# Earlier loads in the opening and an untouched memory input: one decoder layer on one core

## The chip, the cores and the metric

The kernel runs on one core of a Trainium2 chip. The core has a tensor engine (PE, with its weight loads shown as PEld), a vector engine (DVE), a scalar engine (ACT), GpSimd (POOL) and a sync engine (SP), which here issues most DMAs. Each engine works through its own instructions in a fixed order and waits, where it must, on semaphores of the others. The metric is the device time of one execution in microseconds (us); the median over several executions is compared.

## The reference

One layer of a hybrid decoder for a prompt of 1024 tokens and 8 sample tokens (1032 columns together), model width 1024, in float32. What matters here:

```python
def rmsnorm(x, w, eps=RMS_EPS):
    xf = x.astype(jnp.float32)
    y = xf * lax.rsqrt(jnp.mean(xf * xf, axis=-1, keepdims=True) + eps)
    return (y * w.astype(jnp.float32)).astype(x.dtype)
...
    sc_b, sc_c, sc_x, z, xbc, dt_raw, q, gates = jnp.split(xn @ w_in, splits, axis=-1)
...
    xbc_c = jax.nn.silu(xbc_c + ssm_conv_b)
...
    dt = jax.nn.softplus(dt_raw.astype(jnp.float32) + ssm_dt_bias.astype(jnp.float32))
    a = -jnp.exp(ssm_a_log.astype(jnp.float32))
...
        mem_n = rmsnorm(mem_prompt, norm_mem_w[l])
        mk = (mem_n @ w_mem_k[l]).reshape(bp, MEM_LEN, ATTN_HEADS, ATTN_HEAD_DIM)
        mv = (mem_n @ w_mem_v[l]).reshape(bp, MEM_LEN, ATTN_HEADS, ATTN_HEAD_DIM)
```

`xn` is the normalized input. It is multiplied by the columns of `w_in`; of these the change touches z (a SiLU gate), xBC (a causal convolution of width 4, which for the sample tokens needs the stored histories) and dt. Keys and values come from 256 normalized memory tokens.

## The kernel before

Matrices are cut into blocks of 128 columns. A product in full precision is made from three products in a faster type: a number is split into a rounded part (tile names ending in h, made by a copy on ACT) and the rest (ending in l, made by a subtraction on DVE), and h·h, h·l and l·h are added up in PSUM. One block of 128 output columns is `gemm`: 8 slices of the inner dimension, three products each, 24 groups; a group is three matmuls of 512, 256 and 264 columns (L220). `weights` (L159) loads a block of weights into a tile with the tag `raw`, of which there are three, and splits it.

*Opening* (L447 to L608). The rows of x come in by DMA in three thirds (`g3` = 0, 1, 2). PE turns each 128x128 block (`ps_xt`), ACT copies it to `xt` (five buffers), SP stores that to `xT_d`, DVE scales it into `xw`, ACT and DVE split it into `xnh` and `xnl`. Products with the dt columns (`ps_dt`) and with the first block of B (`ps_B0`) run among this. Behind the opening come the histories: four DMAs, 32 small transposes (`ps_h`) and four copies on DVE (L610 to L622).

*The next stage* (L1245 to L1253). The block C0 is multiplied (`ps_C`), then z0 and z1 (`z_step`, L854), then pairs of z blocks by a Strassen scheme (`z_pair`, tiles named Z2, Z4 and so on, L266). At the same time DVE and ACT have four things to do: the convolutions of B0 and C0 (`conv`, L745); the sums and differences of quarters of xn that the Strassen scheme needs (`make_raw` and `make_forms`, L1217 to L1234; tiles T1, nT2, T4 and `raw3`); the splitting of weights; and the chain for dt: `dtr` (bias added, read from `ps_dt`), softplus in some twenty operations on [128, 288] (`dt_softplus`), which ends in `dtT` and `da`, and then on PE `ps_ac` (running sums of `da`, `dt_sums`), `ps_acT` (`dt_rows`) and `ps_ex` (`dt_sample`).

*Memory tokens* (L1263 to L1317). Two tiles of 128 tokens are loaded, squared and summed on ACT, multiplied by the root of their mean square on DVE, turned by PE (`mem_t`, `ps_mt`), and each 128x128 piece is scaled by `norm_mem_w` and split, by ACT for the h part and by DVE for the l part. `kv_block` multiplies them with the key and value weights (`ps_kv`) and ACT copies the result out.

The order on each engine is decided when the program is built: a scheduler takes the program in the order in which it was written, plays it through with its own estimates of durations, and puts on each engine whatever is ready by these. Steps in the list `pend` (the dt chain, the memory steps) are written into the products by `tick`, between slices. `tc.issue_after(ins)` is a rule for this scheduler: what is written in the block comes, on the engine of `ins`, behind `ins`.

Two tiles of three PSUM banks (`mm_ps`, tag mm) serve the big products. `ps_dt` and `ps_B0` hold both through the opening; `ps_C` gets one when `dtr` has read `ps_dt` or the copy `uB` has read `ps_B0`, and z0 and z1 get the next ones.

Of the kernel before, what the change touches and what calls it, by code (L numbers as in the profile page):

```python
# [17 lines left out]
P = 128  # L18
# [29 lines left out]
def tile_kernel(ctx: ExitStack, tc, a, o):  # L48
# [123 lines left out]
    def ev_tile(name, shape=(P, TT + 4), dt=F32):  # L172
        return ev.tile(list(shape), dt, tag="ev", name=name)
# [289 lines left out]
    with tc.tile_pool(name="p0", bufs=1) as p0:  # L463
# [123 lines left out]
        root_of(0)  # L587
        for g3 in range(3):
            c, n_all = span(g3)
            for k in range(KD):  # L590
                ps = sm_ps(f"ps_xt{g3}{k}")
                blocks(g3, ps, lambda i, t, n: t[:, k * P : (k + 1) * P])
                ins = to_xn(k, c, ps, n_all, f"{g3}{k}")
                if g3 < 2 and 1 <= k < 1 + len(srcs[g3 + 1]):
                    with tc.issue_after(ins):
                        square(g3 + 1, k - 1)
                if g3 == 0 and k == 2:
                    first_weights()
                if g3 > 0 or k > 3:
                    products.popleft()()  # L600
                if g3 < 2 and k == 5:
                    root_of(g3 + 1)
        while products:
            products.popleft()()
        for k in range(KD):
            b_product(2, k)

        SY.dma_start(r_d, rbc[0:1, :])  # L608


    for src, dst, nr, nt in (
        (a["state_ssm_conv"][0].rearrange("b j c -> (b j) c"), h_xc, 24, 24),
        (a["state_conv"][0].rearrange("b j c -> (b j) c"), h_sc, 16, 8),
    ):
        per = 8
        for q0 in range(0, nt, per):
            t = ev_tile(f"hist{nr}_{q0}", (nr, per * P))
            SY.dma_start(t, src[:, q0 * P : (q0 + per) * P])
            ps = sm_ps(f"ps_h{nr}_{q0}")
            for i in range(per):  # L620
                PE.transpose(ps[:, i * nr : (i + 1) * nr], t[:, i * P : (i + 1) * P], ident[:nr, :nr])
            V.tensor_copy(dst[:, q0 : q0 + per, :].rearrange("p a b -> p (a b)"), ps[:, : per * nr])  # L622
# [16 lines left out]
    bias = pd_.tile([2 * HEADS, 1], F32, tag="bias", name="bias")
    V.memset(bias, 0.0)  # L640
    SY.dma_start(bias[:HEADS], a["ssm_dt_bias"].rearrange("l h -> h l"))
    dtr = ev_tile("dtr", (2 * HEADS, TT))
    V.tensor_scalar(dtr[:, :TT], flat(ps_dt)[: 2 * HEADS], bias, None, op0=ALU.add)
# [10 lines left out]
    def dt_softplus():  # L654
        ps = sm_ps("ps_dtT")
        for c in range(NCK):
            PE.transpose(
                ps[:, c * 2 * HEADS : (c + 1) * 2 * HEADS], dtr[:, c * P : (c + 1) * P], ident[: 2 * HEADS, : 2 * HEADS]
            )
        pss = sm_ps("ps_dtS")  # L660
        PE.transpose(pss[:NS, : 2 * HEADS], dtr[:, T:TT], ident[: 2 * HEADS, : 2 * HEADS])
        V.memset(x0[:, 256:], 0.0)
        for dst, src in ((x0[:, :256], ps), (x0[:NS, 256:], pss[:NS, : 2 * HEADS])):
            dst = dst.rearrange("p (c h) -> p c h", h=HEADS)
            src = src.rearrange("p (c t h) -> p c t h", t=2, h=HEADS)
            V.tensor_copy(dst, src[:, :, 0])
            V.tensor_tensor(dst, src[:, :, 1], dst, op=ALU.add)
        V.tensor_scalar(mx, x0, 0.0, None, op0=ALU.max)
        V.scalar_tensor_tensor(u, x0, -1.0, x0, op0=ALU.mult, op1=ALU.min)
        S.activation(u, u, AF.Exp)  # L670
        V.tensor_scalar(z, u, 2.0, None, op0=ALU.add)
        V.reciprocal(z, z)
        V.tensor_mul(z, z, u)
        V.tensor_mul(z2, z, z)
        V.tensor_scalar(q, z2, 1.0 / 17.0, None, op0=ALU.mult)
        for n in (15, 13, 11, 9, 7, 5, 3):
            V.scalar_tensor_tensor(q, q, 1.0 / n, z2, op0=ALU.add, op1=ALU.mult)
        V.scalar_tensor_tensor(q, q, 1.0, z, op0=ALU.add, op1=ALU.mult)
        V.scalar_tensor_tensor(dt_flat, q, 2.0, mx, op0=ALU.mult, op1=ALU.add)
        abc = pd_.tile([P, HEADS], F32, tag="abc", name="abc")  # L680
        SY.dma_start(abc, a["ssm_a_log"][0:1, :].to_broadcast([P, HEADS]))
        S.activation(abc, abc, AF.Exp)
        V.scalar_tensor_tensor(
            da, dtT, -1.0, bc(abc.unsqueeze(1), [P, 9, HEADS]), op0=ALU.mult, op1=ALU.mult
        )
# [32 lines left out]
    def dt_sample():  # L718

        esm = pd_.tile([NS, HEADS], F32, tag="esm", name="esm")  # L720
        S.activation(esm, da[:NS, 8, :], AF.Exp)
        exp2 = pd_.tile([16, 2], F32, tag="exp2", name="exp2")
        SY.dma_start(exp2, a["ssm_d"].rearrange("l (t two) -> (l t) two", two=2))
        ex = pd_.tile([16, 2, 64], F32, tag="ex", name="ex")
        V.tensor_copy(ex, bc(exp2.unsqueeze(2), [16, 2, 64]))
# [12 lines left out]
        V.tensor_copy(es.rearrange("p t b -> p (t b)"), ps[:, 128:256])  # L738
        V.tensor_copy(dpar, ps[:, 256:272])


    def proj(col, name):
        return gemm(weights(wblock(w_in, col), "w" + name), xn, "ps_" + name)

    def conv(acc, u, hist, key, ct, nt, taps, bias):  # L745

        w = [par(key, j * nt + ct) for j in range(taps)]
# [2 lines left out]
        if bias is None:  # L750
            S.activation(acc[:, :T], u[:, 0:T], AF.Copy, scale=w[0])
            V.tensor_scalar(ap_s, hv[:, :, 0], w[0], None, op0=ALU.mult)
        else:
            S.activation(acc[:, :T], u[:, 0:T], AF.Identity, scale=w[0], bias=bias)
# [472 lines left out]
    def make_forms(k0):  # L1227
        mk = fx_tile if k0 == 0 else act_pair
        raws = [make_raw(kt) for kt in (k0, k0 + 1)]
        for i, f in enumerate(("T1", "nT2", "T4")):  # L1230
            form_tiles(f, k0, mk)
            for kt in (k0, k0 + 1):
# [9 lines left out]
            V.scalar_tensor_tensor(b12, b12, par("mix", kt), rb[:, HS[1]], op0=ALU.mult, op1=ALU.mult)  # L1242
        return ts

    w_c0 = weights(wblock(w_in, C_XBC + 20 * P), "wC0")  # L1245
    xbc_tile(16, "B0", ps_b0)
    make_forms(0)
    xbc_tile(20, "C0", w=w_c0)
    make_forms(2)
    z_step(0)  # L1250
    flush()
    dt_stack.close()
    mem_stack = ExitStack()  # L1253
# [14 lines left out]
            SY.dma_start(t, a["mem_prompt"][0, m * P : (m + 1) * P, :])  # L1268
            mem_sb.append(t)

    def mem_rms():
        for m in range(2):
            junk = memT[m][0].rearrange("p k c -> p (k c)")
            S.activation(junk, mem_sb[m], AF.Square, accum_out=mst[:, m : m + 1])
        rsqrt(pm, mrs, mst, D, [P, 2], "m")
        for m in range(2):
            V.tensor_scalar(mem_sb[m], mem_sb[m], mrs[:, m : m + 1], None, op0=ALU.mult)

    def mem_t(m, half):
        hi, lo = memT[m]  # L1280
        ps = sm_ps(f"ps_mt{m}{half}")
        for k4 in range(4):
            k = half * 4 + k4
            PE.transpose(ps[:, k4 * P : (k4 + 1) * P], mem_sb[m][:, k * P : (k + 1) * P], ident)
        for k4 in range(4):
            k = half * 4 + k4
            pk = ps[:, k4 * P : (k4 + 1) * P]
            S.activation(hi[:, k, :], pk, AF.Copy, scale=par("mem", k))
            V.scalar_tensor_tensor(
                lo[:, k, :], pk, par("mem", k), f32(hi)[:, k, :], op0=ALU.mult, op1=ALU.subtract  # L1290
            )

    pss_kv = []

    def kv_block(j, q):
# [16 lines left out]
            return  # L1312
        t = ev_tile(f"kv{j}", (P, 2, 256))
        for m in range(2):
            S.copy(t[:, m, :], pss_kv[m][:, :256])
# [4 lines left out]
    pend.extend([None, mem_rms, None])  # L1320
    pend.extend(lambda m=m, half=half: mem_t(m, half) for m in range(2) for half in range(2))
    pend.extend(lambda j=j, q=q: kv_block(j, q) for j in range(8) for q in range(2))
    pace[0] = 5
    z_step(1)
# [774 lines left out]
```

## Time and profile before

| | |
|---|---|
| median of 3 executions | 2475.04 us (2474.16 to 2475.89) |
| profiled execution, its time | 2474.8 us |
| profiled execution, its span | 2472.7 us |
| PE busy | 2428.5 us (98%) |
| DVE busy | 1584.3 us (64%) |
| ACT busy | 1067.1 us (43%) |
| mean granted PE clock | 0.994 |

The profile is one execution seen by the hardware profiler. Its views are the chain of work that ended last, tables of who waited for whom, a timeline of instructions, groups of instructions with their mean duration, and tables by stretch of time. A line such as L220 is a line of the kernel; a name such as `ps_C` is the tile written, with buffer numbers left out. In the timeline a row's "us" runs from the first start to the last end of the instructions merged in it, so neighbouring rows may overlap by a little; differences of starts are used where that matters.

### The profile page before, as it was taken

How to read it: one execution, taken by the hardware profiler on the slowest of the kernel's cores; microseconds unless marked ns; L12 is line 12 of the kernel's file. 1: busy time of each engine (PE TensorE's matmuls, PEld its weight loads, DVE VectorE, ACT ScalarE, POOL GpSimd, SP SyncE). 2: the span in 40 equal slices, each digit the busy share in tenths (PEclk: the TensorE clock that was granted, in tenths of full speed). 3: DMA queues.
4: the chain of work that ended last, by engine and by line, in shares of the span. 5: the costliest groups of instructions: out<-in, count | busy, mean ns of one | idle time of the engine just before them, and what ended most of it. 6: DMA issues, size and time to landing. Idle time of an engine off the chain costs nothing.

```text
span 2472.7 us, 45688 instructions
## 1 busy us (share of the span) xinstructions
PE 2428.5 (98%) x18946; PEld 2310.5 (93%) x18946; DVE 1584.3 (64%) x2601; ACT 1067.1 (43%) x1712; POOL 114.8 (5%) x163
## 2 busy tenths in 40 slices
PE   8999999999999999999999999999999999999998
PEld 6899999999999999888888888899999999999998
DVE  6844586777677774666767562454787555476755
ACT  6654455354545535556545441223453333342322
POOL 0100000000000000121120000000000000000000
PEclk8999999999999999999999999999999999999999
DMA  6344434344344456667878677874454323264421
GB/s 195 121 139 154 132 102 153 112 130 131 108 137 137 129 154 210 194 207 254 265 219 286 205 265 238 266 241 153 141 174 134 108 86 112 74 231 132 156 85 69
DMA packets 359662, 404.42 MB, mean 164 GB/s; under 512 B 17446, under 2 KB 286870, under 8 KB 359447
## 3 DMA queue, kind: packets, MB, share of 16 engines
q1 hardware_dynamic: 339006, 343.79, 44.6%
q10 hardware_dynamic: 20449, 57.71, 6.0%
q8 instruction: 149, 2.44, 0.4%
q14 instruction: 58, 0.48, 0.1%
HBM read 286.35 MB, written 115.32 MB: 162 GB/s over the span
## 4 chain that ended last, share of the span: by engine, by line
PE 86%; DMA 5%; DVE 5%; ACT 2%; issue 1%; SPq 0%; ACTq 0%; POOL 0%; DVEq 0%
PE po L220 12%; PE ps_q L220 4%; PE pm L1800 3%; PE ps_g L220 2%; PE pd L220 1%; PE py L1041 1%; PE pss L1054 1%; PE po L1033 1%; PE Z2m L266 1%; PE Z4m L266 1%; PE X8m L266 1%; PE d12m L266 1%; PE C2m L266 1%; PE C4m L266 1%; PE G18m L266 1%
## 5 line engine op out<-in xcount | busy, mean ns | idle before, releaser
L986 ACT ACTIVATE r<-r,acum 128x128 f32<-128x128 f32 x256 | 79.2, 392 | 5.1 <-DMA r<-ac_d 4.7
L757 DVE SCALAR_TENSOR_TENSOR ax<-u,prm,ax 128x1024 f32<-128x1024 f32 x44 | 56.3, 1279 | 0.0
L927 ACT ACTIVATE st<-st,es 128x128 f32<-128x128 f32 x128 | 41.5, 392 | 26.4 <-DMA st<-in_state_ssm_dram 23.9
L1018 POOL TENSOR_TENSOR xdd<-xdt,decst 128x512 f32<-128x512 f32 x32 | 37.1, 1160 | 292.2 <-DVE xdt L1014 292.2
L1447 DVE TENSOR_TENSOR yr<-po,yr 128x1032 f32<-128x1032 f32 x8 | 9.8, 1230 | 55.1 <-PE po L220 45.2
L1037 DVE TENSOR_TENSOR y<-po,ea 128x512 f32<-128x512 f32 x28 | 19.3, 690 | 38.9 <-PE po L1033 38.9
L1012 DVE TENSOR_TENSOR r<-r,cbm 128x1024 f32<-128x1024 f32 x32 | 39.2, 1224 | 2.5
L929 DVE SCALAR_TENSOR_TENSOR st<-sr,dts,st 128x128 f32<-128x128 f32 x128 | 40.3, 345 | 0.4
L1011 ACT COPY bT<-bp 128x128 f32<-128x128 f32 x32 | 8.5, 265 | 64.3 <-DVE cbm L1009 64.2
L2034 ACT ACTIVATE fj<-psy 128x512 f32<-128x512 f32 (+1 forms) x18 | 10.7, 596 | 59.1 <-PE psy L2032 59.0
L933 DVE SCALAR_TENSOR_TENSOR sr<-st,sr 128x128 f32<-128x128 f32 x128 | 35.2, 285 | 1.1
L1054 PE MATMUL pss<-xdd,bT 128*128 128x512 f32 x64 | 33.4, 604 | 2.3 <-ACT bT L1011 2.3
L1041 PE MATMUL py<-r,xdt 128*64 128x128 f32 x512 | 35.0, 279 | 0.0
L987 ACT ACTIVATE r<-r 128x1024 f32<-128x1024 f32 x32 | 33.9, 1058 | 0.7
L1014 DVE TENSOR_TENSOR xdt<-xp,dtT 128x512 f32<-128x512 f32 x32 | 21.9, 684 | 18.7 <-PE xp L1007 18.5
L1807 DVE TENSOR_TENSOR x<-pm,xT 128x516 f32<-128x516 f32 x16 | 11.1, 695 | 35.1 <-PE pm L1800 35.1
L1067 POOL TENSOR_TENSOR s<-s,cdec 128x512 f32<-128x512 f32 x28 | 32.1, 1145 | 4.5 <-DVE s L1060 3.9
L1041 PEld LDWEIGHTS py<-r,xdt 128*64 128x64 f32 x512 | 27.3, 136 | 4.2 <-issue 0.5
L1033 PE MATMUL po<-bc,s 128*128 128x128 f32 x224 | 29.6, 275 | 0.0
L760 DVE SCALAR_TENSOR_TENSOR ax<-u,prm,ax 128x1032 f32<-128x1032 f32 x22 | 28.3, 1286 | 0.0
L1178 DVE SCALAR_TENSOR_TENSOR x<-x,prm,sqa 128x1032 f32<-128x1032 f32 x16 | 19.7, 1288 | 13.3 <-ACT sqa L1174 13.3
L1033 PEld LDWEIGHTS po<-bc,s 128*128 128x128 f32 x224 | 27.7, 191 | 0.5
(9066 smaller groups left out, 9044.0 us busy)
## 6 DMA issues: line engine op xcount, KB each, us to landing
r<-ac_d SPq DMA_DIRECT2D x32, 512.0 KB
gt<-gt_d SPq DMA_DIRECT2D x24, 516.0 KB
xs_d<-ax ACTq DMA_DIRECT2D x22, 516.0 KB
gt_d<-G ACTq DMA_DIRECT2D x20, 516.0 KB
x<-xs_d SPq DMA_DIRECT2D x16, 516.0 KB
zs<-zs_d SPq DMA_DIRECT2D x16, 516.0 KB
yb_d<-x SPq DMA_DIRECT2D x16, 516.0 KB
in<-yb_d SPq DMA_DIRECT2D x16, 516.0 KB
```

The costliest lines, as they stand in the source:

```text
L220: PE.matmul(out[:, c : c + n], wt[:, ks], x[:, c : c + n], start=(k == 0 and i == 0), stop=(k == nk - 1 and i == 2),)
L266: PE.matmul(hv(ps)[:, c : c + n], wt[:, ks], x[:, c : c + n], start=(start and kt == 0 and i == 0), stop=(kt == 3 and i == 2), skip_group_ ...
L757: V.scalar_tensor_tensor(acc[:, :T], u[:, j : j + T], w[j], acc[:, :T], op0=ALU.mult, op1=ALU.add)
L927: S.activation(st[:, i], st[:, i], AF.Copy, scale=es[:, g * 4 + i, b : b + 1])
L929: V.scalar_tensor_tensor(st[:, i], rb, dts[:, g * 4 + i, b : b + 1], st[:, i], op0=ALU.mult, op1=ALU.add)
L986: S.activation(r[:, j, :], r[:, j, :], AF.Relu, scale=-1.0, bias=acum[:, c, h : h + 1])
L1012: V.tensor_tensor(r, r, bc(cbm.unsqueeze(1), [P, HPG, P]), op=ALU.mult)
L1018: G.tensor_tensor(b3(xdd, HPG), b3(xdt, HPG), bc(decst[:, c, hs].unsqueeze(2), [P, HPG, 64]), op=ALU.mult)
L1033: PE.matmul(po[:, t * P : (t + 1) * P], state["s"][:, t * P : (t + 1) * P], bcg[1][:, cs], start=True, stop=True,)
L1041: PE.matmul(py[hp : hp + 64, (h // 2) * P : (h // 2 + 1) * P], xdt[:, h * 64 : (h + 1) * 64], r[:, (h % 2) * 4 + h // 2, :], start=True, s ...
L1054: PE.matmul(pss, bT, xdd, start=True, stop=True)
L1800: PE.matmul(hv(ps)[:, c : c + n], wt[:, ks], x[:, half * HT + c : half * HT + c + n], start=(k == 0 and i == 0), stop=(k == KD - 1 and i = ...
```

## The change

The change has three parts.

*Opening.* The loads of wC0 (at the second third), of wz0, wz1 and the four histories (at the last third), and of the three small tensors bias, abc and exp2 (ahead of the first third) are moved into the opening. `dtr` and the splitting of wC0 are now written into the end of the opening, with a rule that wC0's split comes behind `dtr` on DVE and behind the last split of xn on ACT. The histories' transposes stay behind it in the text.

*Order behind it.* `make_raw` for the first pair is written before the forms, and the forms, C0 and the z products come behind the last history copy on DVE and behind B0's first convolution step on ACT.

*Memory.* The tokens are no longer multiplied by the root. They are turned raw, multiplied by `norm_mem_w` in one operation of 512 columns that writes back into `mem`, and split by one cast and one subtraction per half. The root is applied when keys and values are copied out of PSUM, as a scale per token.

```diff
+        bias = cn.tile([2 * HEADS, 1], F32, tag="bias", name="bias")
+        V.memset(bias, 0.0)
+        SY.dma_start(bias[:HEADS], a["ssm_dt_bias"].rearrange("l h -> h l"))
...
         for g3 in range(3):
             c, n_all = span(g3)
+            if g3 == 1:
+                loaded["wC0"] = load_raw(wblock(w_in, C_XBC + 20 * P), "wC0")
+            if g3 == 2:
+                for i in range(2):
+                    loaded[f"wz{i}"] = load_raw(wblock(w_in, C_Z + i * P), f"wz{i}")
+                for src, dst, nr, nt in past_of:
+                    for q0 in range(0, nt, 8):
+                        t = ev_tile(f"hist{nr}_{q0}", (nr, 8 * P))
+                        SY.dma_start(t, src[:, q0 * P : (q0 + 8) * P])
+                        hists.append((t, dst, nr, q0))
...
+        dtr = ev_tile("dtr", (2 * HEADS, TT))
+        turned = V.tensor_scalar(dtr[:, :TT], flat(ps_dt)[: 2 * HEADS], bias, None, op0=ALU.add).ins
+        with tc.issue_after(turned), tc.issue_after(ins):
+            w_c0 = weights(None, "wC0")
...
-        S.activation(abc, abc, AF.Exp)
+        with tc.issue_after(ex_u):
+            S.activation(abc, abc, AF.Exp)
...
-    w_c0 = weights(wblock(w_in, C_XBC + 20 * P), "wC0")
     xbc_tile(16, "B0", ps_b0)
-    make_forms(0)
-    xbc_tile(20, "C0", w=w_c0)
-    make_forms(2)
-    z_step(0)
+    raws = [make_raw(kt) for kt in (0, 1)]
+    with tc.issue_after(past), tc.issue_after(tap[0]):
+        make_forms(0, raws)
+        xbc_tile(20, "C0", w=w_c0)
+        make_forms(2)
+        z_step(0)
...
-    def mem_rms():
+    def mem_squares():
         for m in range(2):
             junk = memT[m][0].rearrange("p k c -> p (k c)")
             S.activation(junk, mem_sb[m], AF.Square, accum_out=mst[:, m : m + 1])
+
+    def mem_root():
         rsqrt(pm, mrs, mst, D, [P, 2], "m")
-        for m in range(2):
-            V.tensor_scalar(mem_sb[m], mem_sb[m], mrs[:, m : m + 1], None, op0=ALU.mult)
...
-        for k4 in range(4):
-            k = half * 4 + k4
-            pk = ps[:, k4 * P : (k4 + 1) * P]
-            S.activation(hi[:, k, :], pk, AF.Copy, scale=par("mem", k))
-            V.scalar_tensor_tensor(
-                lo[:, k, :], pk, par("mem", k), f32(hi)[:, k, :], op0=ALU.mult, op1=ALU.subtract
-            )
+        ks = slice(half * 4, half * 4 + 4)
+        w = prm[:, PC["mem"] + half * 4 : PC["mem"] + half * 4 + 4]
+        t = b3(mem_sb[m][:, half * 512 : half * 512 + 512], 4)
+        V.tensor_tensor(t, b3(ps, 4), bc(w.unsqueeze(2), [P, 4, P]), op=ALU.mult)
+        S.copy(hi[:, ks], t)
+        V.tensor_sub(lo[:, ks], t, f32(hi[:, ks]))
...
-            S.copy(t[:, m, :], pss_kv[m][:, :256])
+            S.activation(t[:, m, :], pss_kv[m][:, :256], AF.Copy, scale=mrs[:, m : m + 1])
```

The scheduler puts the instructions elsewhere as a result. Three places follow as they stand in the built program: the line, the operation, the tile written, the tiles read, the shape written. First PE around `ps_ac`, before: this is in the middle of z1, when z0 is complete.

```order
L220 MATMUL ps_z1_1105<-xnh4_162,wz1h_1101 128x512
L220 MATMUL ps_z1_1105<-xnh4_162,wz1h_1101 128x256
L220 MATMUL ps_z1_1105<-xnh4_162,wz1h_1101 128x264
L690 MATMUL ps_ac_851<-da_716,tri_82 128x256
L691 MATMUL ps_ac_851<-da_716,ones_80 128x256
L220 MATMUL ps_z1_1105<-xnl4_163,wz1h_1101 128x512
L220 MATMUL ps_z1_1105<-xnl4_163,wz1h_1101 128x256
L220 MATMUL ps_z1_1105<-xnl4_163,wz1h_1101 128x264
```

And the same place of the change. Ahead of these rows stand C0 and two groups of z0 (xnh0 and xnl0 with wz0h).

```order
L220 MATMUL ps_z1_1105<-xnh0_154,wz1h_1101 128x512
L220 MATMUL ps_z1_1105<-xnh0_154,wz1h_1101 128x256
L220 MATMUL ps_z1_1105<-xnh0_154,wz1h_1101 128x264
L220 MATMUL ps_z1_1105<-xnl0_155,wz1h_1101 128x512
L220 MATMUL ps_z1_1105<-xnl0_155,wz1h_1101 128x256
L220 MATMUL ps_z1_1105<-xnl0_155,wz1h_1101 128x264
L704 MATMUL ps_ac_857<-da_730,tri_82 128x256
L705 MATMUL ps_ac_857<-da_730,ones_80 128x256
L220 MATMUL ps_z0_937<-xnh0_154,wz0l_934 128x512
L220 MATMUL ps_z0_937<-xnh0_154,wz0l_934 128x256
L220 MATMUL ps_z0_937<-xnh0_154,wz0l_934 128x264
```

`ps_ac` has moved from behind 37 of the 48 groups of z0 and z1 to behind 4 of them; the first product with wz0l stands behind it. Second, DVE where wz0l is made, before: at the start of this stage, right behind wC0l and dtr.

```order
L169 TENSOR_TENSOR wC0l_723<-wC0r_720,wC0h_722 128x1024
L643 TENSOR_SCALAR dtr_708<-ps_dt_178,bias_705 64x1032
L755 TENSOR_SCALAR aB0_730<-h_xc_153,prm_119 128x8
L169 TENSOR_TENSOR wz0l_930<-wz0r_927,wz0h_929 128x1024
L758 SCALAR_TENSOR_TENSOR aB0_730<-h_xc_153,prm_119,aB0_730 128x8
L725 COPY ex_981<-exp2_979 16x128
```

And of the change, where the dt chain ends.

```order
L693 SCALAR_TENSOR_TENSOR q_729<-q_729,z_727 128x288
L417 TENSOR_TENSOR T42al_928<-xw6_176,T42ah_927 128x516
L694 SCALAR_TENSOR_TENSOR dtT_713<-q_729,mx_725 128x288
L417 TENSOR_TENSOR T42al_928<-xw7_177,T42ah_927 128x516
L697 SCALAR_TENSOR_TENSOR da_730<-dtT_713,abc_227 128x288
L169 TENSOR_TENSOR wz0l_934<-wz0r_510,wz0h_933 128x1024
L737 COPY ex_983<-exp2_229 16x128
L169 TENSOR_TENSOR wz1l_1102<-wz1r_512,wz1h_1101 128x1024
L707 COPY acum_712<-ps_ac_857 128x256
```

wz0l has moved from the third operation behind wC0l to the one behind `da`, with the whole of the convolutions, forms and softplus in front of it; wz1l, which stood among the forms, follows it. Third, SP at the end of the opening, before.

```order
L531 DMA xT_d_120<-xt26_589 128x264
L531 DMA xT_d_120<-xt27_601 128x264
L140 DMA wC0r_720<-in_w_in_dram 128x8x128
L140 DMA wz0r_927<-in_w_in_dram 128x8x128
L641 DMA bias_705<-in_ssm_dt_bias_dram 32x1
L681 DMA abc_820<-in_ssm_a_log_dram 128x32
L723 DMA exp2_979<-in_ssm_d_dram 16x2
L140 DMA wz1r_1099<-in_w_in_dram 128x8x128
```

And of the change, the stores of the opening's first and second third.

```order
L544 DMA xT_d_120<-xt06_346 128x384
L140 DMA wC0r_372<-in_w_in_dram 128x8x128
L544 DMA xT_d_120<-xt07_361 128x384
L544 DMA xT_d_120<-xt10_378 128x384
L544 DMA xT_d_120<-xt11_393 128x384
L140 DMA wz0r_510<-in_w_in_dram 128x8x128
L544 DMA xT_d_120<-xt12_409 128x384
L140 DMA wz1r_512<-in_w_in_dram 128x8x128
```

The three weight loads now stand among the stores; bias, abc and exp2 stand ahead of the first store.

More of the change, by code (lines that the diff above doesn't have):

```diff
@@ L525, in tile_kernel @@
         SY.dma_start(xs_sb, a["x_sample"][:, 0, :])
+        bias = cn.tile([2 * HEADS, 1], F32, tag="bias", name="bias")
+        V.memset(bias, 0.0)
+        SY.dma_start(bias[:HEADS], a["ssm_dt_bias"].rearrange("l h -> h l"))
+        abc = cn.tile([P, HEADS], F32, tag="abc", name="abc")
+        SY.dma_start(abc, a["ssm_a_log"][0:1, :].to_broadcast([P, HEADS]))
+        exp2 = cn.tile([16, 2], F32, tag="exp2", name="exp2")
+        SY.dma_start(exp2, a["ssm_d"].rearrange("l (t two) -> (l t) two", two=2))
+        past_of = (
+            (a["state_ssm_conv"][0].rearrange("b j c -> (b j) c"), h_xc, 24, 24),
+            (a["state_conv"][0].rearrange("b j c -> (b j) c"), h_sc, 16, 8),
+        )
+        hists = []
         def to_xn(k, c, ps, n, name):
@@ L608, in tile_kernel @@
         SY.dma_start(r_d, rbc[0:1, :])
[L611 to L622, printed above, removed]
+    for t, dst, nr, q0 in hists:
+        ps = sm_ps(f"ps_h{nr}_{q0}")
+        for i in range(8):
+            PE.transpose(ps[:, i * nr : (i + 1) * nr], t[:, i * P : (i + 1) * P], ident[:nr, :nr])
+        past = V.tensor_copy(dst[:, q0 : q0 + 8, :].rearrange("p a b -> p (a b)"), ps[:, : 8 * nr]).ins
     SY.dma_start(o["s_conv"][0, :, 0, :], a["state_conv"][0, :, 1, :])
@@ L638, in tile_kernel @@
     pd_ = dt_stack.enter_context(tc.tile_pool(name="pdt", bufs=1))
[L639 to L643, printed above, removed]
     W = 9 * HEADS
@@ L669, in dt_softplus @@
         V.scalar_tensor_tensor(u, x0, -1.0, x0, op0=ALU.mult, op1=ALU.min)
-        S.activation(u, u, AF.Exp)
+        ex_u = S.activation(u, u, AF.Exp).ins
         V.tensor_scalar(z, u, 2.0, None, op0=ALU.add)
@@ L679, in dt_softplus @@
         V.scalar_tensor_tensor(dt_flat, q, 2.0, mx, op0=ALU.mult, op1=ALU.add)
-        abc = pd_.tile([P, HEADS], F32, tag="abc", name="abc")
-        SY.dma_start(abc, a["ssm_a_log"][0:1, :].to_broadcast([P, HEADS]))
-        S.activation(abc, abc, AF.Exp)
+        with tc.issue_after(ex_u):
+            S.activation(abc, abc, AF.Exp)
         V.scalar_tensor_tensor(
@@ L721, in dt_sample @@
         S.activation(esm, da[:NS, 8, :], AF.Exp)
-        exp2 = pd_.tile([16, 2], F32, tag="exp2", name="exp2")
-        SY.dma_start(exp2, a["ssm_d"].rearrange("l (t two) -> (l t) two", two=2))
         ex = pd_.tile([16, 2, 64], F32, tag="ex", name="ex")
@@ L743, in proj @@
         return gemm(weights(wblock(w_in, col), "w" + name), xn, "ps_" + name)
+    tap = []
     def conv(acc, u, hist, key, ct, nt, taps, bias):
@@ L753, in conv @@
         else:
-            S.activation(acc[:, :T], u[:, 0:T], AF.Identity, scale=w[0], bias=bias)
+            tap[:] = [S.activation(acc[:, :T], u[:, 0:T], AF.Identity, scale=w[0], bias=bias).ins]
             V.tensor_scalar(ap_s, hv[:, :, 0], w[0], bias, op0=ALU.mult, op1=ALU.add)
@@ L1225, in make_raw, with make_forms @@
         return b11, b22, b21
-    def make_forms(k0):
+    def make_forms(k0, raws=None):
         mk = fx_tile if k0 == 0 else act_pair
-        raws = [make_raw(kt) for kt in (k0, k0 + 1)]
+        raws = raws or [make_raw(kt) for kt in (k0, k0 + 1)]
         for i, f in enumerate(("T1", "nT2", "T4")):
@@ L1319, in tile_kernel @@
     mem_load()
-    pend.extend([None, mem_rms, None])
+    pend.extend([None, mem_squares])
     pend.extend(lambda m=m, half=half: mem_t(m, half) for m in range(2) for half in range(2))
+    pend.append(mem_root)
     pend.extend(lambda j=j, q=q: kv_block(j, q) for j in range(8) for q in range(2))
```

## The prediction

> **What bounds the kernel now.** First the chain of work that ended last, by engine, from the page:
>
> ```profile
> span 2472.7 us, 45688 instructions
> PE 86%; DMA 5%; DVE 5%; ACT 2%; issue 1%; SPq 0%; ACTq 0%; POOL 0%; DVEq 0%
> ```
>
> The tensor engine (PE) sets the end. All that the change touches lies in the first 270 us, mostly in the first 140, so I asked next whom PE waited for between 50 and 140 us (total, times, longest), and what clock it had after those waits (the table of stretches: stretch, its length, PE busy with its instructions, PEld, DVE, ACT, POOL, then the granted clock):
>
> ```profile
> PE ps_C L220 <- ACT uB L837: 4.2, 1, 4.2
> PE ps_mt L1284 <- DVE meml L1289: 2.1, 1, 2.1
> PE Z2m L266 <- ACT z L858: 1.6, 1, 1.6
> PE Z4m L266 <- ACT Z4Sh L253: 0.5, 1, 0.5
> 58.00:60.00 2.00, 1.27 (x4) 1.21 (x5) 2.00 (x5) 1.97 (x3) 1.26 (x2) 0.50 0.97 272
> 60.00:62.00 2.00, 2.00 (x8) 1.71 (x8) 2.00 (x6) 2.00 (x3) 0.00 (x1) 0.50 1.10 281
> 62.00:64.00 2.00, 2.00 (x18) 1.77 (x16) 2.00 (x3) 0.92 (x3) 0.00 (x0) 0.89 0.76 204
> 126.00:128.00 2.00, 1.39 (x8) 1.15 (x8) 1.84 (x3) 2.00 (x6) 0.00 (x0) 0.82 0.01 2
> 128.00:130.00 2.00, 2.00 (x11) 2.00 (x11) 1.56 (x4) 1.98 (x8) 0.00 (x0) 0.50 0.00 0
> 130.00:132.00 2.00, 2.00 (x16) 2.00 (x16) 1.61 (x6) 1.60 (x6) 0.00 (x0) 0.82 0.00 0
> ```
>
> Four waits, 8.4 us in all. Behind the first the clock is 0.50: lost are 1.27 × 0.50 + 2 × 0.50 + 2 × 0.11 = 1.9 us. Around the second it dips again: 2 × (0.18 + 0.50 + 0.18) = 1.7 us. So all that this part can give is 8.4 + 1.9 + 1.7 = 12 us. Next, PE's own landmarks in the timeline (start, duration, what, and in brackets the idle time before):
>
> ```profile
> 52.20 2.28 PE L621 MATMUL ps_h<-ident,hist 24*128 24x24 f32 x32
> 58.73 1.20 PE L220 MATMUL ps_C<-xnh,wC0h 128*128 128x512 f32 x3 [4.25 <-ACT uB L837]
> 72.69 0.63 PE L220 MATMUL ps_z<-xnh,wz0h 128*128 128x512 f32 x3
> 83.97 0.63 PE L220 MATMUL ps_z<-xnh,wz1h 128*128 128x512 f32 x3
> 90.07 0.59 PE L690 MATMUL ps_ac<-da,tri 128*128 128x256 f32 x2
> 98.74 0.50 PE L266 MATMUL Z2m<-xnh,Z2Ah 128*128 128x256 f32 x2 [1.60 <-ACT z L858]
> ```
>
> z0's 24 groups of three products take 83.97 - 72.69 = 11.28 us: **0.47 us a group**. When ps_ac starts at 90.07, z0 is done, and 13 of z1's 24 groups. Then the vector engine (DVE) in the same stretch, its waits first:
>
> ```profile
> DVE h_xc L622 <- PE ps_h L621: 2.0, 2, 1.8
> DVE acum L693 <- PE ps_ac L691: 0.5, 1, 0.5
> 54.03 0.36 DVE L622 COPY h_xc<-ps_h 128x192 f32<-128x192 f32 x1 [0.27 <-PE ps_h L621]
> 54.52 0.29 DVE L622 COPY h_sc<-ps_h 128x128 f32<-128x128 f32 x1
> 56.17 1.22 DVE L169 TENSOR_TENSOR wC0l<-wC0r,wC0h 128x1024 fp32r<-128x1024 f32 x1
> 57.31 1.28 DVE L643 TENSOR_SCALAR dtr<-ps_dt,bias 64x1032 f32<-64x1032 f32 x1
> 58.70 1.21 DVE L169 TENSOR_TENSOR wz0l<-wz0r,wz0h 128x1024 fp32r<-128x1024 f32 x1
> 59.98 0.21 DVE L725 COPY ex<-exp 16x128 f32<-16x128 f32 x1
> 72.58 1.21 DVE L169 TENSOR_TENSOR wz1l<-wz1r,wz1h 128x1024 fp32r<-128x1024 f32 x1
> 88.97 0.45 DVE L683 SCALAR_TENSOR_TENSOR da<-dtT,abc 128x288 f32<-128x288 f32 x1
> 89.33 1.29 DVE L417 TENSOR_TENSOR T42al<-xw,T42ah 128x516 fp32r<-128x516 f32 x2
> ```
>
> Its only waits between 50 and 92 us are for the histories' transposes, before 55 us, and for ps_ac behind `da`. From wC0l at 56.17 to the end of da at 89.42 it works without a gap: **33.25 us of vector work**. PE does not feel this, since it has C0, z0 and half of z1 to do meanwhile.
>
> **The change part by part.** *Loads and histories.* wC0, wz0, wz1, the histories and the three small tensors are asked for some 20 us earlier, so the landing of wC0 no longer holds anything. What is late next is the reading of the first two PSUM tiles: dtr from ps_dt, uB from ps_B0. By the changed order ten history transposes (10 × 2.28 / 32 = 0.7 us) and two small products come after the last one into ps_dt. The opening's PE work is unchanged, to 52.20 + 2.28 = 54.5, so ps_dt is full at some 53.5; dtr takes 1.28, and C0 starts at **54.8 instead of 58.73**. Nearly no idle time lies before it, so the 0.50 clock goes with the 4.2 us.
>
> More is queued on SP in the opening: three small DMAs go ahead of the first store to xT_d, three weight loads and the histories among the stores. A store waits for earlier loads already, and the sixth copy into `xt` needs the first store's buffer back:
>
> ```profile
> SPq L531 <- DMA x<-in_x_prompt_dram: 1.5, 2, 0.9
> 23.84 0.48 ACT L530 COPY xt<-ps_xt 128x384 f32<-128x384 f32 x1 [2.69 <-PE ps_xt L549]
> ```
>
> ACT is idle 2.7 us there, waiting for PE; that covers a later store. I take 0. Without this cover it would be the 1.5 us of the first row again; on the other side 0.5 us can be gained, since two of four 516-wide subtractions leave the opening's end on DVE.
>
> *The z products behind da.* This carries the forecast. In the changed order PE does C0, two groups of z0 and two of z1, then ps_ac, and only then z0's third group, which needs wz0l. DVE makes wz0l directly behind da. So all of da's 33 us now stand in front of 44 of the 48 z groups. When is da ready? From wC0l on DVE has the 33.25 us of before, without dtr (1.28, now ahead), wz0l, wz1l (1.21 each) and ex (0.21), and with both history copies (0.36 + 0.29) and three pairs of 516-wide operations (T10al, xw, T42al: 1.29 a pair by the T42al row): 33.25 - 3.91 + 0.65 + 3.87 = **33.9 us**. wC0l follows dtr at 54.8, so da ends at 88.7, as before within a microsecond. PE arrives far earlier: 13.96 us for C0 (72.69 - 58.73) less the 1.9 of slow clock is 12.1, so C0 ends at 66.9, the four z groups (1.9 us) at 68.8. **PE then waits some 20 us for da.**
>
> The sum, against before at the same work: ps_ac starts 90.07 - 88.7 = 1.3 us earlier (-1.3), but with 4 groups of z done, not 37: 33 × 0.47 = +15.5. After so long a wait the clock starts low: +1.9 as after the 4.2 us wait. No wait of over 4.2 us is in the trace, so this price has bounds of 0 and twice that, 3.8; I take the nearest row.
>
> A rule to weigh here: the Trainium skill, "TensorE: Matmul & The Clock Gate", Part 1, says that one idle window of about 3.4 us halves the clock, and some 3.4 us of steady work restores it, however long the idleness was. As an estimate from that page the price would be 1.7 us, and the sum 11.1 in place of 11.3. By the same rule the 2.1 us wait at 125 us would be too short to slow the clock; yet 0.50 stands behind it in 128 to 130, so here the trace decides, and were the rule right about that dip, its 1.7 us would stay and the sum be 13.0.
>
> *Memory tokens.* Before, 16 pieces go to and fro between ACT and DVE, and the product that waited 2.1 us waits for them:
>
> ```profile
> L1288 ACT ACTIVATE memh<-ps_mt,prm 128x128 fp32r<-128x128 f32 x15 | 5.0, 368 | 0.6 <-DVE meml L1289 0.6
> L1289 DVE SCALAR_TENSOR_TENSOR meml<-ps_mt,prm,memh 128x128 fp32r<-128x128 f32 x15 | 4.8, 346 | 2.5 <-ACT memh L1288 2.5
> L395 DVE TENSOR_TENSOR Z<-Z,Z2m 128x516 f32<-128x516 f32 x1 | 0.7, 693 | 0.5 <-PE Z2m L266 0.5
> L1315 ACT COPY kv<-ps_kv x16: 372/373/389, 141.0 to 270.5; 128x256 f32<-128x256 f32 x16
> ```
>
> Now there are four multiplications of 128x512 (nearest row 0.69 us each), four casts and four subtractions, and PE's transposes come earlier, among z1's last groups, with the root off the path. The 2.1 us wait, the 0.5 us behind it and the dip of 1.7 should go. The 1.6 us wait of Z2m for z1's SiLU loses the 0.5 us of the four transposes that now stand between. Together -4.8. The root at keys and values turns 16 copies of 373 ns into ACTIVATEs with a scale; the nearest such row is 368 ns on half the columns, so one costs 0 to some 0.35 us more, up to 5.6 us in all, on an ACT that waits for PE there: I take 0 for the end. The transposes, products and their sizes stay the same.
>
> Sum: -1.3 + 15.5 + 1.9 - 4.8 = **+11.3 us**. Later stages are bound by PE and move as a whole. The profiled execution took 2474.8 us (span 2472.7; the median of the three runs is 2475.0, the same within 0.01%), so I expect **2486 us**.
>
> **The rivals.** *The later waits stay.* The new multiplication overwrites mem in place and must wait for the squares on ACT, which stand behind the four casts of raw3; one PSUM slot further PE waits for it. If this takes the place of the old wait, 4.3 us are not won: 11.3 + 4.3 = 15.6, 2490 us. For it: a dozen operations of this part now stand before Z2m on ACT and DVE; against: z1's last groups on PE cover them.
>
> *Faster: the vector work is not in front.* If da were ready by 69 us, PE would run through: -3.9 (C0) - 1.9 (clock) - 4.8 = -10.6, 2464 us. This decides from da at 77.4 (88.7 - 11.3): earlier is faster. The vector work would have to shrink from 33.9 to 22.6 us. For it speaks only that da's own operations are a part of it; against, that DVE shows no gap in the 33 us of before, and that the changed order puts the same operations ahead.
>
> *The stall is half as long*, since ACT and DVE, no longer starved in the opening, finish earlier: da near 77, about 2475 us. Nothing in the rows shows where 11 us should come from.
>
> **How the numbers follow.** Likeliest 0.76; the waits that stay 0.15; the half stall 0.05; faster 0.04. The likeliest case's own bounds: the clock free (-1.9), the opening quicker (-0.5), the Z2m wait gone (-1.1) give +7.8; the clock doubled (+1.9) and the opening's 1.5 give +14.7. For 8 in 10 I take **2480 to 2492**, which holds the second case and leaves out the rest. About 0.2% (5 us) is what a measurement of this kernel tells from no change; slower by more than that 0.91, within it 0.05, faster 0.04.
>
> **What would show it.** Right: one PE wait of 17 to 21 us before ps_ac, released by da on DVE; DVE without a gap from wC0l to da, da's end between 87 and 90; clock 0.50 in the 4 us behind; C0 starting near 55 at full clock; no wait of ps_mt over 1 us. Wrong: da before 80, a PE wait under 10 us there, or new PE waits after 120 us.

## The result and the profile after

| | us |
|---|---|
| before, median of 4 executions beside the changed kernel | 2475.47 (2474.16 to 2477.91) |
| changed kernel, median of 4 executions | 2489.07 (2488.64 to 2489.82) |
| ratio, with its 95% interval | 1.0054 (1.0037 to 1.0072) |
| changed kernel, profiled execution, its span | 2488.1 |

The changed kernel is slower by 13.6 us. The prediction was 2486 us (2480 to 2492): slower by 11.

First the page of the changed kernel, its span and the chain that ended last by engine:

```profile
span 2488.1 us, 45666 instructions
PE 86%; DVE 5%; DMA 5%; ACT 2%; issue 2%; SPq 0%; ACTq 0%; DVEq 0%; POOL 0%
```

PE sets the end as before. Whom it waited for between 50 and 170 us (total, times, longest):

```profile
PE ps_ac L704 <- issue: 19.2, 1, 19.2
PE Z2m L266 <- ACT z L872: 1.3, 1, 1.3
PE ps_C L220 <- ACT uB L851: 0.4, 1, 0.4
PE ps_z L220 <- ACT uC L851: 0.2, 1, 0.2
```

Before, there were four waits of 8.4 us in all, the longest of 4.2. Now one of 19.2 us stands for nearly all. The table says "issue": the profile shows no releaser for it. The timeline of PE, DVE and ACT tells who came last:

```profile
54.88 0.74 PE L220 MATMUL ps_C<-xnh,wC0h 128*128 128x512 f32 x3 [0.39 <-ACT uB L851]
68.95 0.63 PE L220 MATMUL ps_z<-xnh,wz0h 128*128 128x512 f32 x3
72.28 1.28 DVE L771 SCALAR_TENSOR_TENSOR aC<-uC,prm,aC 128x1024 f32<-128x1024 f32 x1 [1.93 <-ACT aC L768]
90.03 0.45 DVE L697 SCALAR_TENSOR_TENSOR da<-dtT,abc 128x288 f32<-128x288 f32 x1
90.40 1.22 DVE L169 TENSOR_TENSOR wz0l<-wz0r,wz0h 128x1024 fp32r<-128x1024 f32 x1
90.58 1.19 PE L704 MATMUL ps_ac<-da,tri 128*128 128x256 f32 x2 [19.16 <-issue]
92.06 1.42 PE L220 MATMUL ps_z<-xnh,wz0l 128*128 128x512 f32 x3
```

C0 starts at 54.88, not 58.73. Then DVE ends `da` at 90.48, PE starts `ps_ac` 0.1 us later, and behind it come wz0l and the first product that reads it. The table of stretches shows the clock at C0, behind the long wait, and where the memory tokens had cost something before:

```profile
56.00:58.00 2.00, 2.00 (x8) 1.77 (x8) 2.00 (x6) 2.00 (x4) 0.08 (x2) 0.53 0.29 52
58.00:60.00 2.00, 2.00 (x12) 1.65 (x12) 2.00 (x4) 1.98 (x3) 0.00 (x0) 0.62 0.71 210
90.00:92.00 2.00, 1.42 (x4) 1.17 (x5) 2.00 (x5) 0.23 (x1) 1.67 (x1) 0.50 0.76 224
92.00:94.00 2.00, 2.00 (x9) 1.72 (x8) 2.00 (x3) 0.00 (x0) 0.00 (x0) 0.59 0.92 260
128.00:130.00 2.00, 2.00 (x19) 2.00 (x18) 1.08 (x1) 1.35 (x5) 0.00 (x0) 1.00 0.74 214
```

The dip at 126 to 132 us is gone, and with it the waits of `ps_mt` and Z4m. But 1.2 us behind C0's start the clock falls to one half, from 56.1 to 59.5 us, though only 0.39 us of waiting stand before C0.

### The profile page after: what moved, and what is told of

It reads as the page before. It is cut to its first block, busy times and chain, and to the rows that moved or that the text cites. A ratio compares the mean times of both kernels' runs of the same rounds, so it can differ in the third digit from the quotient of the medians.

```text
span 2488.1 us, 45666 instructions
## 1 busy us (share of the span) xinstructions
PE 2429.5 (98%) x18946; PEld 2310.8 (93%) x18946; DVE 1583.7 (64%) x2591; ACT 1063.5 (43%) x1699; POOL 121.2 (5%) x163
## 4 chain that ended last, share of the span: by engine, by line
PE 86%; DVE 5%; DMA 5%; ACT 2%; issue 2%; SPq 0%; ACTq 0%; DVEq 0%; POOL 0%
PE po L220 12%; PE ps_q L220 4%; PE pm L1815 3%; PE ps_g L220 2%; PE pd L220 1%; PE py L1055 1%; PE pss L1068 1%; PE po L1047 1%; PE ps_z L220 1%; PE Z2m L266 1%; PE G8m L266 1%; PE C3m L266 1%; PE G18m L266 1%; PE Z14m L266 1%; PE C6m L266 1%
## 5 line engine op out<-in xcount | busy, mean ns | idle before, releaser
L1001 ACT ACTIVATE r<-r 128x1024 f32<-128x1024 f32 x32 | 33.8, 1058 | 0.7
L1744 DVE TENSOR_TENSOR gt<-po,gt 128x1032 f32<-128x1032 f32 x8 | 9.9, 1232 | 29.6 <-PE po L220 27.3
```

## The experiments

Two theories stood at the start. **A**: the loss is PE's wait for `da`, which comes of the place of wz0l and wz1l on DVE. **B**: it comes from the rest, the moved loads or the memory edit.

**e1 and e2: the splits early, in the changed kernel.** `weights` for z0 and z1 (e1), or for z0 alone (e2), is written ahead of the forms; the scheduler then puts the subtractions there too.

```diff
...
     with tc.issue_after(past), tc.issue_after(tap[0]):
+        w_z = [weights(None, f"wz{i}") for i in range(2)]
         make_forms(0, raws)
         xbc_tile(20, "C0", w=w_c0)
         make_forms(2)
-        z_step(0)
+        z_step(0, w_z[0])
...
-    z_step(1)
+    z_step(1, w_z[1])
```

> The changed kernel, but the casts and subtractions of wz0 and wz1 are written ahead of make_forms(0), so that DVE makes wz0l and wz1l before the forms and before da; PE then has all 48 z groups ahead of ps_ac. Theory A (the loss is PE waiting for da because wz0l stands behind it): PE's wait of 19.2 us before ps_ac shrinks to 0-3 us: C0 ends at 69.1, 48 groups of 0.47 us end at 91.7, da ends at 90.5 + 2.4 = 92.9. About 2468 us (2464 to 2472), faster than both kernels. Rival B (the opening's moved loads or the memory edit cost the time): 2485 us or more. Rival C (the vector work is the bound, so the wait only moves to the Z2 products): 2475 to 2482 us.

> The changed kernel, with only wz0's cast and subtraction written ahead of make_forms(0). PE then has z0 and two groups of z1 ahead of ps_ac. Theory A: those 26 groups end at 69.1 + 12.2 = 81.3, da ends at 90.5 + 1.2 = 91.7, a wait of about 10 us is left with 22 z groups behind it: about 2479 us (2476 to 2482), between the two others. Rival B (the time is lost elsewhere): unchanged near 2489 us.

e1: 2469.91 us, ratio to before 0.9975 (0.9965 to 0.9984). e2: 2478.27 us, 1.0009 (1.0001 to 1.0018). Both are within 2 us of what theory A said, and B is out: both kernels keep the moved loads and the memory edit, and e1 is faster than before. PE's longest wait of e2 between 50 and 170 us, then the two longest of e1:

```profile
PE ps_ac L704 <- issue: 8.9, 1, 8.9
```

```profile
PE Z2m L266 <- ACT Z2Sh L253: 1.0, 1, 1.0
PE ps_acT L723 <- ACT cdec L711: 0.5, 1, 0.5
```

19.2, 8.9, none: the wait shrinks as PE may do 4, 26 or 48 z groups before `ps_ac`. In e1's timeline wz0l stands at 63 us, and `da` is still done at 89.2 (expected had been 92.9). The two subtractions cost DVE 2.4 us ahead of `da`, but its gap of 1.93 us is not there in e1, and the last two subtractions for T42al (1.28 us), which stood ahead of `da`, now stand behind it:

```profile
63.16 1.21 DVE L169 TENSOR_TENSOR wz0l<-wz0r,wz0h 128x1024 fp32r<-128x1024 f32 x1
64.90 1.21 DVE L169 TENSOR_TENSOR wz1l<-wz1r,wz1h 128x1024 fp32r<-128x1024 f32 x1
88.75 0.44 DVE L697 SCALAR_TENSOR_TENSOR da<-dtT,abc 128x288 f32<-128x288 f32 x1
89.63 0.59 PE L704 MATMUL ps_ac<-da,tri 128*128 128x256 f32 x2
```

**e4: the splits late, in the kernel before.** The reverse: one rule, nothing else of the change.

```diff
...
+    with tc.issue_after(da_at[0]):
+        w_z = [weights(wblock(w_in, C_Z + i * P), f"wz{i}") for i in range(2)]
-    z_step(0)
+    z_step(0, w_z[0])
...
```

> The kernel before, with one edit: the casts and subtractions of wz0 and wz1 may not be issued before da, as it comes out in the changed kernel. Theory A: this alone makes the loss. da ends at 89.4 - 2.4 = 87.0, PE comes to ps_ac after C0 (72.7) and 4 z groups (74.6) and waits 12.4 us, then 44 z groups: -3.1 + 33 x 0.47 + 1.9 of slow clock = +14.3, about 2490 us (2486 to 2493). Rival B (the place of the splits is not the cause): 2474 to 2478 us.

2490.08 us, ratio 1.0058 (1.0044 to 1.0071): +14.4 us, as expected. PE's longest waits between 50 and 170 us:

```profile
PE ps_ac L692 <- issue: 13.9, 1, 13.9
PE ps_C L220 <- ACT uB L839: 4.3, 1, 4.3
PE ps_z L220 <- ACT uC L839: 2.4, 1, 2.4
```

The place of the splits alone makes a loss as large as the change's. The single terms agree less well than the sum: in the profiled execution, the longest of the six (2496.89 us), `da` ends at 91.5 us, not at 87.0, mainly because DVE waits 1.5 us for a load and 2.4 us for ACT on the way. That the medians differ by just the expected amount is partly luck.

**e3: the memory edit alone, on the kernel before.** `mem_squares`, `mem_root`, the new `mem_t` and the scale at the key and value copies are as in the change.

> The kernel before with the memory edit alone (tokens turned raw, one multiplication of 512 columns, root at keys and values). Theory A: the wait of ps_mt (2.1 us), of Z4m (0.5), the dip of the clock at 126-132 us (1.7) and 0.5 of Z2m's wait go: 2475.5 - 4.8 = 2470.7 us (2469 to 2473). Rival (the scale at the key and value copies costs up to 0.35 us on each of 16, or the waits stay): 2474 to 2481 us.

2470.28 us, ratio 0.9975 (0.9961 to 0.9988): -5.4 us. The waits of `ps_mt` and Z4m are gone, that of Z2m stays at 1.6 us. The scale costs ACT 97 ns a copy (470 ns in the changed kernel's row below, 373 before), and no wait of PE shows it:

```profile
L1329 ACT ACTIVATE kv<-ps_kv,mrs x16: 465/470/476, 149.8 to 284.6; 128x256 f32<-128x256 f32 x16
```

**e9: the opening alone.** The changed kernel with the old memory steps. My theory said that the parts add up.

> The changed kernel with the memory edit undone: the opening, the raws made ahead and their order rules stay. Theory A (the parts add up: the opening's order costs, the memory edit alone gave 5.2 us in e3): 2489.1 + 5.2 = 2494 us (2491 to 2497), PE's wait before ps_ac again 19 to 20 us, the products into ps_kv still 283 ns. Rival (the 19 us wait comes from both parts together, so that without the memory edit the splits' place does no harm): below 2485 us.

2487.99 us, ratio 1.0051 (1.0034 to 1.0067), where 2494 was expected: a **miss**. The memory edit gains nothing behind this opening. At the first product of X0, behind this part, the profiles with and without it stand at 347.2 and 347.4 us. Two of PE's waits say why:

```profile
PE ps_ac L704 <- issue: 19.1, 1, 19.1
PE ps_mt L1299 <- DVE mem L1292: 0.3, 1, 0.3
```

While PE stands still for 19 us, DVE and ACT go on; the old, slower memory steps then are on time, with a wait of 0.3 us where before's order had 2.1 us.

**e10 and e11: the memory edit with the wait mended.** If that is so, the edit must count again once the splits are early. e11 is the best kernel so far (e1 with the memory tiles moved, e5 below); e10 is the same with the old memory steps.

> The kernel of e5 with the memory edit undone (tokens scaled by the root first, 16 pieces to and fro between ACT and DVE). In e9 the opening's 19 us wait of PE let ACT and DVE get ahead, so that the old memory steps were never late there and the memory edit gave nothing. Here that wait is gone. Theory J (the memory edit is worth its 5 us only where PE has not waited before): the waits of ps_mt and Z4m come back, 2465.4 + 5 = 2470 us (2468 to 2473). Rival (once the splits are early, the memory steps have slack in any case): 2465 to 2467 us.

> The kernel of e5 once more beside e10, to compare on one chip: both splits early, memory tiles at a multiple of 128 bytes, memory edit kept. 2465.4 us as before (2463 to 2468), 1.0 % to 0.3 % under the kernel before.

e11: 2466.41 us, 0.9953 (0.9941 to 0.9965). e10: 2477.88 us, 0.9997 (0.9987 to 1.0006). The sign is theory J's, but the size, 11.5 us, is twice the expected and e10 lies outside its expected range. PE's longest waits of e10 between 50 and 170 us:

```profile
PE ps_mt L1300 <- DVE mem L1293: 3.8, 1, 3.8
PE Z4m L266 <- ACT Z4Ah L253: 3.2, 1, 3.2
```

And the stretch around them, at half clock for nearly its whole length:

```profile
121.50:131.75 10.25, 7.07 (x33) 6.55 (x33) 6.52 (x16) 8.87 (x26) 0.00 (x0) 0.51 0.13 52
```

Waits of 7.0 us (e11 has 0.7 for Z4m and none for `ps_mt`), and PE busy for 7.07 us at half clock, which is 3.5 us lost: together 9.8 of the 11.5. (At the first product of X0 the two profiles are only 333.9 - 326.3 = 7.6 us apart, partly because e11's profile has half clock at C0, 54.4 to 57.8 us, and e10's has not.) So one edit is worth 5.4 us on the old order, nothing behind a 19 us stall, and 11.5 us once PE runs ahead.

**e5, e6, e7: where the memory tiles lie.** The products into `ps_kv` took longer in the changed kernel than before, though nothing was meant to change in them. Each line of the tile's own view gives least, median and greatest ns of eight products, and their first and last start; here the second blocks of j = 1 and j = 7, before:

```profile
L1308 PE MATMUL ps_kv<-wkv11h,memh x8: 276/276/280, 154.8 to 157.2; 128*128 128x256 f32 x8
L1308 PE MATMUL ps_kv<-wkv71h,memh x8: 276/276/280, 267.5 to 269.9; 128*128 128x256 f32 x8
```

And after:

```profile
L1322 PE MATMUL ps_kv<-wkv11h,memh x8: 280/283/283, 167.1 to 169.6; 128*128 128x256 f32 x8
L1322 PE MATMUL ps_kv<-wkv71h,memh x8: 280/283/283, 281.5 to 284.0; 128*128 128x256 f32 x8
```

From the one block to the other PE needs 267.5 - 154.8 = 112.7 us before and 281.5 - 167.1 = 114.4 after, 1.7 us more with no wait between.

In the built programs the memory tiles start at byte 187008 before and at 187200 after, since bias, abc and exp2 changed pools: a multiple of 128 in the one, 64 above one in the other. e5 is e1 with these tiles 64 bytes higher:

```diff
-    mst = pm.tile([P, 2], F32, tag="mst", name="mst")
+    mst = pm.tile([P, 24], F32, tag="mst", name="mst")[:, :2]
```

> The kernel of e1 with one edit: the tile mst takes 96 bytes in place of 32, so that the four tiles memh/meml start 64 bytes higher, at a multiple of 128 bytes, as in the kernel before. In the traces of the changed kernel, e1 and e2 the 384 products into ps_kv (stationary operand memh or meml) take 283 ns and PE falls back 1.7 us between ps_kv of j=1 and of j=7; in before, e3 and e4 they take 276 ns and it does not. The opening's three small tiles, moved to another pool, shift those tiles by 192 bytes. Theory D (the 64-byte offset of the stationary operand is the cause): ps_kv products back at 276 ns, 1.7 us less than e1: about 2468.2 us. Rival E (something else in the opening's order is the cause, such as DMA traffic): 283 ns stays, 2470 us.

2465.38 us, ratio 0.9958 (0.9944 to 0.9971). The products are back at the time of before:

```profile
L1323 PE MATMUL ps_kv<-wkv11h,memh x8: 276/276/280, 145.6 to 148.0; 128*128 128x256 f32 x8
L1323 PE MATMUL ps_kv<-wkv71h,memh x8: 276/276/280, 258.5 to 260.9; 128*128 128x256 f32 x8
```

The stretch takes 258.5 - 145.6 = 112.9 us (e1: 263.1 - 148.7 = 114.4): the place of these tiles is the cause. Of the 4.5 us between the medians of e1 and e5 the products of this stretch explain 1.5; the ranges of the two overlap (2464.3 to 2475.7 and 2462.6 to 2467.1). The clock accounts for much of the rest in the profiled executions: between 100 and 2400 us that of e1 (2475.7 us) has 20.5 us at half clock, that of e5 (2462.6) none, and PE loses half of such a time, some 10 us. e6 asks whether all weights gain by it:

```diff
-    cp = ctx.enter_context(tc.tile_pool(name="const", bufs=1))
     wp = ctx.enter_context(tc.tile_pool(name="weights", bufs=3))
+    cp = ctx.enter_context(tc.tile_pool(name="const", bufs=1))
```

> The kernel of e5 with one edit: the pool of weights is allocated ahead of the pool of constants, so every tile of split weights starts at a multiple of 128 bytes, not 64 above one; no engine's order changes. These tiles are the stationary operand of 16,248 of PE's products. Theory D for every product: each starts 4.5 to 6 ns sooner (1.7 us over 288 products of ps_kv give 5.9), so 70 to 95 us less where PE is the bound: about 2385 us (2370 to 2405). Rival F (the offset costs only in ps_kv, or only the products of 256 columns show it): 256- and 260-column products alone would give up to some 60 us, none of it 2468 us, as e5.

2469.19 us, ratio 0.9977 (0.9967 to 0.9986): a **clear miss**, 84 us off. The products of Z8 keep their 281 or 282 ns, and those into `ps_kv`, whose memory tiles lie as in e5, become slow again, for now the moving operand wkv lies at a multiple of 128 too:

```profile
L1323 PE MATMUL ps_kv<-wkv41h,memh x8: 277/283/283, 203.0 to 205.5; 128*128 128x256 f32 x8
```

So it is not the stationary operand alone. Fast was memory at a multiple of 128 with wkv 64 above one; both 64 above (after), and both at a multiple (e6), were slow. e7 puts the four tiles at four offsets:

```diff
-        (pm.tile([P, KD, P], F32R, tag=f"mh{m}", name=f"memh{m}"), pm.tile([P, KD, P], F32R, tag=f"ml{m}", name=f"meml{m}"))
+        [
+            pm.tile([P, D + 8], F32R, tag=f"m{p}{m}", name=f"mem{'AB'[m]}{p}")[:, :D].rearrange("p (k c) -> p k c", k=KD)
+            for p in "hl"
+        ]
```

> The kernel before, with the four memory tiles at four offsets from a multiple of 128 bytes: memAh 0, memAl 32, memBh 64, memBl 96 (eight columns more in each tile, nothing else). Theory D: the products into ps_kv with memAh take 276 ns, those with memBh 283; 32 and 96 tell whether a 512-byte row that is not at a multiple of 128 bytes costs the same (283) or more. Rival E: all 276 ns, as in before.

One execution, 2480.55 us. The products with memAh, at offset 0, do not take 276 ns either (the view ends at 216 us and holds three products of each):

```profile
L1311 PE MATMUL ps_kv<-wkv41h,memAh x3: 280/280/282, 214.0 to 215.4; 128*128 128x256 f32 x3
L1311 PE MATMUL ps_kv<-wkv41h,memBh x3: 277/278/283, 214.3 to 215.8; 128*128 128x256 f32 x3
```

That speaks against theory D's simple form and doesn't give another; which pairs of offsets are slow, and why, stays open.

**e8: the clock at C0.** The changed kernel once more, one execution.

> The changed kernel once more, nothing edited, for the clock at C0's start, where the prediction erred. Theory G (the clock is set for stretches of 3.4 us that lie anyhow against the program, so the same sparse stretch of PE at 52 to 55 us, small transposes and a wait of 0.4 us, now halves the next stretch and now does not): the wait before ps_ac again 19 to 20 us, but the half clock at C0 begins at another time than 56.1 us, or does not come; it lasts 3.4 us or a multiple of it. Rival H (the half clock at 56.1 to 59.5 us belongs to the order of the work): the same place again to 0.3 us.

2490.69 us; PE's wait is again 19.1 us. The table in quarters of a microsecond tells where the half clock begins and ends, first in the first profile of the changed kernel, then in this one:

```profile
56.00:56.25 0.25, 0.25 (x2) 0.21 (x2) 0.25 (x2) 0.25 (x2) 0.08 (x2) 0.72 0.00 0
59.50:59.75 0.25, 0.25 (x3) 0.09 (x3) 0.25 (x1) 0.25 (x1) 0.00 (x0) 0.95 0.05 12
```

```profile
54.00:54.25 0.25, 0.25 (x5) 0.15 (x3) 0.25 (x1) 0.25 (x1) 0.00 (x0) 0.95 0.00 0
57.50:57.75 0.25, 0.25 (x3) 0.21 (x2) 0.25 (x3) 0.25 (x1) 0.00 (x0) 0.73 0.81 113
```

It is slow from 56.1 to 59.5 in one and from 54.2 to 57.6 in the other: 3.4 us each, in another place of the same program. e1, with the same work there and the same 0.39 us wait, shows no dip at all in the table of stretches:

```profile
54.00:56.00 2.00, 1.61 (x11) 1.27 (x10) 2.00 (x4) 1.92 (x3) 1.18 (x2) 1.00 0.00 0
56.00:58.00 2.00, 2.00 (x15) 1.69 (x15) 2.00 (x5) 2.00 (x3) 0.00 (x0) 1.00 0.44 95
```

e5 and e11 are one and the same kernel in two executions: e5 has no dip at C0, e11 has one from 54.4 to 57.8 us. First e5, then e11:

```profile
54.00:56.00 2.00, 2.00 (x13) 1.71 (x12) 2.00 (x5) 2.00 (x3) 0.83 (x2) 1.00 0.03 9
```

```profile
54.00:56.00 2.00, 1.61 (x10) 1.42 (x9) 2.00 (x3) 1.92 (x3) 1.18 (x2) 0.59 0.00 0
```

That is theory G.

## Why the prediction was nearly right

**The long wait** (17 to 21 us, released by `da`): 19.2 us, right, and shown from both sides by e1, e2 and e4. C0's start was to be 54.8 and was 54.88. Both ends of the wait came some 2 us later than foreseen, PE at 71.4 instead of 68.8 and `da` at 90.5 instead of 88.7; the two delays have one cause, the slow clock in C0, so the length held.

**da without a gap on DVE, at 88.7**: off by 1.8 us, and outside the 87 to 90 named as a sign. The work itself, 33.9 us, was right: wC0l starts at 54.78, and 90.48 - 54.78 - 1.93 = 33.8. DVE has one gap, the 1.93 us shown above: it waits for ACT's `aC`, and ACT could copy `ps_C` only when C0 was done, at 69.1 instead of 66.9.

**C0 at full clock**: wrong, and with it the -1.3 for an earlier `ps_ac`; it came out +0.5 (90.58 against 90.07). The step that failed is "Nearly no idle time lies before it, so the 0.50 clock goes with the 4.2 us". The runs show that idle time alone does not set it (below). e5 and e11, one kernel without and with the dip, show too that these 3.4 us at half clock, 1.7 us of time, depend on the single execution; both executions of the changed kernel that were profiled had them.

**33 groups, +15.5**: right. **The clock behind the long wait, +1.9**: 1.42 × 0.50 + 2 × 0.41 = 1.5 us by the rows above, so the nearest row served. That it came so close is partly luck: in e8, the same kernel, the half clock lasts until 95.2 us and costs 2 × 0.50 + 2 × 0.50 + 2 × 0.30 = 2.6 us behind `ps_ac`, which starts at 89.9. The last two of these three stretches:

```profile
92.00:94.00 2.00, 2.00 (x8) 1.72 (x8) 2.00 (x5) 0.00 (x0) 0.00 (x0) 0.50 0.92 261
94.00:96.00 2.00, 2.00 (x15) 1.77 (x13) 0.38 (x3) 0.69 (x2) 0.00 (x0) 0.70 1.03 311
```

**Memory, -4.8**: the size in the sum was right (2.1 + 0.5 + 1.7 + 0.3 = 4.6 us are gone), the reason only half. The prediction gave it to the memory edit, and e3 shows that on the old order the edit does this; but e9 shows that the opening's own stall takes those waits away without the edit. The rival "the later waits stay" did not come. Its mechanism, PE waiting for the new multiplication, does not show in e11 either, where PE is not held up: there is no wait of `ps_mt`. The waits of e10 are those of the old memory steps.

**Not in the sum**: the products into `ps_kv`, +1.7 us, from three small tiles that changed their pool. The measured terms are 0.5 + 15.5 + 1.5 - 4.6 + 1.7 = +14.6; at the first product of X0, behind this whole part, the profiles stand 347.2 - 333.1 = +14.1 us apart, and the medians 13.6.

## What to carry to other kernels

Where a scheduler sets the order, look for the one small operation that releases the most queued work, here a subtraction of 1.2 us for 44 product groups, and write it early; loading its input early is not enough. Gains of separate edits don't add: a stall on the engine that bounds gives all others time, and hides what a second edit would bring, so test each edit with the others mended. The version with both splits early, the memory edit kept and the memory tiles moved by 64 bytes beats both kernels, by 10 to 12 us against before (e5, e11).

## What the runs showed of the hardware

- **The half clock comes in stretches of a fixed length.** 3.4 us in the rows above; 10.24 us, three times that, in e10; from 73.2 to 93.7 us, six times, around the long wait of the changed kernel. In all 13 profiled executions each stretch lasts 3.41 us or two, three or six times that, but for the last, which the end of the program cuts off. So the price of one and the same wait differs between executions: 1.5 us behind the 19.2 us wait in the first profile of the changed kernel, 2.6 behind the 19.1 us wait in e8. The Trainium skill, "TensorE: Matmul & The Clock Gate", Part 1, says that the window is some 3.4 us long and runs free of the kernel; that agrees.
- **Half clock can follow a stretch in which PE is busy by the profile.** In the 3.41 us ahead of e8's dip PE had no idle time at all; what stands out there are 24 small transposes of histories among the products. The Trainium skill, the same page and Part, has the clock fall after an idle window; this one was not idle. The small transposes alone do not decide it: e1 has 24 of them and no idle time from 50.65 to 54.06 us (stretches of 3.41 us counted back from its dip at 112.1), and no dip behind. What decides stays open. The rows of e8 and of e1 in the table of stretches:

```profile
50.81:54.22 3.41, 3.41 (x36) 2.85 (x34) 1.72 (x4) 1.68 (x3) 0.00 (x0) 1.00 0.23 67
50.65:54.06 3.41, 3.41 (x37) 2.92 (x35) 1.72 (x4) 1.68 (x3) 0.00 (x0) 1.00 0.25 67
```

- **Where tiles lie against each other can cost a product 6 ns of 114.** 24 products into `ps_kv` start over 2.61 us before (211.19 to 213.80) and over 2.74 us after (224.32 to 227.06), with the same shapes and the same clock. The first and the last of them in the timeline of before:

```profile
211.19 0.28 PE L1308 MATMUL ps_kv<-wkv41h,memh 128*128 128x256 f32 x1
213.80 0.28 PE L1310 MATMUL ps_kv<-wkv41l,memh 128*128 128x256 f32 x1
```

And of after:

```profile
224.32 0.28 PE L1322 MATMUL ps_kv<-wkv41h,memh 128*128 128x256 f32 x1
227.06 0.28 PE L1324 MATMUL ps_kv<-wkv41l,memh 128*128 128x256 f32 x1
```
